# One decoder layer in fp32 on one core: side work of the first cross-attention head ordered behind its first query's split, and five weight sums of the second MLP pair given to GpSimd

## The chip, the core and the metric

The kernel runs on one core of one Trainium2 chip. The core has a matrix engine (TensorE, PE in the profile, with PEld for its weight loads), VectorE (DVE), ScalarE (ACT), GpSimd (POOL) and SyncE (SP), which here issues most DMA transfers. Matmul results land in PSUM banks, and everything else stands in SBUF or, between stages, in HBM. The metric is the device time of one execution in microseconds (us), as the median over several runs; lower is better.

## The reference

One layer over 1024 tokens of width 1024, everything in fp32: RMSNorm, a mix of mLSTM heads and forgetting-attention heads, cross-attention of 4 heads into 256 memory tokens, and an MLP with squared ReLU. Cut to what matters:

```
def cross_attention(h, memn, w_q, w_kv, w_o):
    q = (h @ w_q).reshape(B, S, X_HEADS, X_DH)          # 4 heads of 256
    k, v = jnp.split(memn @ w_kv, 2, axis=-1)
    s = jnp.einsum('bqhd,bmhd->bhqm', q, k) * (X_DH ** -0.5)
    p = jax.nn.softmax(s, axis=-1)
    o = jnp.einsum('bhqm,bmhd->bqhd', p, v).reshape(B, S, D)
    return o @ w_o

x = x + cross_attention(rmsnorm(x, ln_x), rmsnorm(mem, ln_mem), w_xq, w_xkv, w_xo)
h = rmsnorm(x, ln2)
x = x + jnp.square(jax.nn.relu(h @ w_ff1)) @ w_ff2      # 1024 -> 4096 -> 1024
```

## The kernel before

**Arithmetic.** An fp32 product is made of three faster matmuls. `split` cuts a tile into a rounded high part, written by ScalarE (L134, or L137 with a scale), and the remainder, written by VectorE (L135, L138). `mm3` then adds low x high, high x low and high x high into one PSUM bank (L186, L187, L188). So each operand passes through ScalarE and VectorE before TensorE can use it. `weights` loads a 128x1024 weight block into a "wr" buffer (two of them, L174) and splits it into "wh" and "wl" (three of each).

**Order.** The program is written as plain Python loops. A scheduler sets the order on each engine from its own estimate of times; `add_manual_dep` with NoSync binds one instruction behind another on the same engine without a semaphore. Each engine runs its instructions strictly in that order, and so does SyncE's queue of transfers.

**Cross attention.** The tokens come in two halves, `hf` 0 and 1 (512 each). For half 0, each head `hd` runs `query_whole(hd)`: the first query block (128 of the head's 256 columns) is summed in bank mm and split to r_b and r_c, the second in bank m2 (m in the profile) and split to r_p and r_a or r_y. It then runs `right_side(hd)`, which serves half 1: it loads two 128x512 rows of x1d into the two "r_f" buffers (L1190), scales them on ScalarE (L1191), and splits 128x256 pieces and differences of them (L134, L135; the differences by GpSimd in `sub`, L1353) into operands of a Strassen-like scheme of seven products. `cross_head` loads the head's keys and values (kxd L1290, vxd L1291), forms the scores in bank sc from them and the query, takes the softmax (L1303 to L1310), transposes (bank tp) and multiplies with the values (bank ov). The next head's first query again needs bank mm.

**MLP.** The first projection is done in pairs of 2x2 blocks with the same seven-product scheme. `left_up(p_, group)` prepares the weights of pair `p_` in three groups: it loads two raw blocks (odd pairs into "wr", even pairs into "z4" buffers), splits them, and forms five sums of 128x512 pieces in place, each needing the one before it. The engine for these sums is `by`. `prepare` calls it LEAD = 5 products ahead. Pairs 0 and 1 run interleaved, later pairs one by one. `left_up` for pair 1 has its first group traced in the last steps of the cross attention's output projection.

Of the kernel before, what the change touches and what calls it, by code (L numbers as in the profile page):

```python
# [44 lines left out]
def hybrid_layer(ctx: ExitStack, tc: tile.TileContext, a: dict, out: bass.AP):  # L45
    nc = tc.nc
    v, s, g = nc.vector, nc.scalar, nc.gpsimd
# [7 lines left out]
    def name(tag):  # L55
        count[0] += 1
        return f"{tag}_{count[0]}"

    def sb(tag, shape, bufs, dt=F32):
        return pool.tile(shape, dt, tag=tag, name=name(tag), bufs=bufs)  # L60

    def act(dt=F32R):
        return sb("act", [P, 8, TH], 7, dt)
# [8 lines left out]
    def w4(shape=(P, 1024), dt=F32):  # L72
        t = sb("w4", [P, 1024], 5, dt)[: shape[0]]
        return t.rearrange("p (a b) -> p a b", b=shape[2]) if len(shape) == 3 else t
# [4 lines left out]
    def w2(tag, n=512, dt=F32, p=P):  # L79
        return sb("r_" + tag, [P, 512], BUFS[tag], dt)[:p, :n]  # L80
# [6 lines left out]
    def ps_tile(tag):  # L87
        return psum.tile([P, 512], F32, tag=tag, name=name(tag), bufs=PBUFS[tag])
# [7 lines left out]
    def ov_():  # L96
        return ps_tile("ov")
# [4 lines left out]
    def mm():  # L102

        tag = banks[turn[0] % len(banks)]
        turn[0] += 1
        return ps_tile(tag)
# [24 lines left out]
    def split(hi, lo, src, scale=None):  # L131

        if scale is None:
            s.activation(hi, src, AF.Copy)  # L134
            return v.tensor_tensor(out=lo, in0=src, in1=hi.bitcast(F32), op=ALU.subtract)  # L135
        else:
            s.activation(hi, src, AF.Copy, scale=scale)  # L137
            return v.scalar_tensor_tensor(out=lo, in0=src, scalar=scale, in1=hi.bitcast(F32), op0=ALU.mult, op1=ALU.subtract)  # L138
# [5 lines left out]
    def in_order(engines=COMPUTE):  # L144
# [5 lines left out]
        for i in traced[start:]:  # L150
# [8 lines left out]
                )  # L159
            last_of[i.engine] = i.name  # L160


    def rotate(*tags):

        spare[tags] = spare.get(tags, -1) + 1
        return w2(tags[spare[tags] % len(tags)])


    def weights(src, n=1024):
        return weight_parts(weight_load(src, n))  # L170

    def weight_load(src, n=1024):
        raw = sb("wr", [P, 1024], 2)[:, :n]
        load(raw, src)  # L174
        return raw

    def weight_parts(raw):
        n = raw.shape[1]
        hi = sb("wh", [P, 1024], 3, F32R)[:, :n]
        lo = sb("wl", [P, 1024], 3, F32R)[:, :n]  # L180
        split(hi, lo, raw)
        return hi, lo

    def mm3(ps, w, x, first, last, more=False):

        nc.tensor.matmul(ps, w[1], x[0], start=first, stop=False, skip_group_check=more)  # L186
        nc.tensor.matmul(ps, w[0], x[1], start=False, stop=False, skip_group_check=more)  # L187
        nc.tensor.matmul(ps, w[0], x[0], start=False, stop=last, skip_group_check=more)  # L188

    def both(pair, f):  # L190
        return f(pair[0]), f(pair[1])
# [66 lines left out]
    def proj(w, x, tiles, kn=KT, order=None, into=None):  # L258

        wv = both(w, lambda t: t.rearrange("p (k c) -> p k c", k=kn))  # L260
        for half, n in order or [(hf, n) for n in range(tiles) for hf in range(2)]:
            ps = mm() if into is None else into
            for k in range(kn):
                mm3(ps, both(wv, lambda t: t[:, k, n * P : (n + 1) * P]), both(x[half], lambda t: t[:, k]), k == 0, k == kn - 1)
            yield n, half, ps

    VEC = {}
    at = 0
# [105 lines left out]
    z, e, q, lf = (small[:, i:j].rearrange("p (t c) -> p t c", c=c) for i, j, c in ((0, 128, GC), (128, 224, GW), (224, 320, GW), (320, 416, GW)))  # L374
# [54 lines left out]
    ps = ov_()  # L429
# [699 lines left out]
    h2 = act(), act()  # L1129
# [3 lines left out]
    def ln_x(n):  # L1133
        return vec[:, VEC["ln_x"] + n :][:, 0:1]
# [13 lines left out]
    def row_second(hf):  # L1148
        rsqrt_sums(x1_accs[hf], rcol[:, 4 * hf : 4 * hf + 4], 4)
        if hf:  # L1150
            to_row(row, rcol, 8, rowd[2:3])

    for n0 in (0, 4):
        ws = [weights(a["w_out_b"][n0 // 2 + i], 6 * P) for i in range(2)]
        for hf in range(2):
            for n in range(n0, n0 + 4):
                w = both(ws[n // 2 % 2], lambda t: t.rearrange("p (k c) -> p k c", k=3)[:, :, n % 2 * P : n % 2 * P + P])
                ps = mm()
# [12 lines left out]
    def right_room(*names):  # L1171
        t = act().rearrange("p a b -> p (a b)").rearrange("p (n q k c) -> p n q k c", n=2, q=2, k=4)
        for e, c in enumerate(names):
            R[c] = t[:, e, 0], t[:, e, 1]
        return t[:, 1]

    def cut_right(c, k, x):
        split(R[c][0][:, k], R[c][1][:, k], x)
# [3 lines left out]
    def right_side(k):  # L1182
        if not fourth:
            for c in (("11", "21"), ("t1", "t2"), ("22", "t3")):
                right_room(*c)
            fourth.append(w4((P, 4, 256)))
        x, y = w2("f"), w2("f")
        for t, n in ((x, k), (y, 4 + k)):
            with tc.issue_after(mix_done[0].ins):
                load(t, x1d[1, :, n])  # L1190
            s.activation(t, t, AF.Copy, scale=ln_x(n))  # L1191
        x1, x2, y1, y2 = (t[:, e * 256 : e * 256 + 256] for t in (x, y) for e in range(2))
        cut_right("11", k, x1)
        cut_right("21", k, y1)
        cut_right("22", k, y2)
        sub(x1, x2, x1, g)
        cut_right("t1", k, x1)
        sub(x1, y2, x1, g)
        cut_right("t2", k, x1)
        sub(x2, y2, x2, g)  # L1200
        cut_right("t3", k, x2)
        sub(fourth[0][:, k], y1, x1, g)

    def q_room(kk):
        return [rotate(*tags).bitcast(F32R) for tags in ((("b",), ("c",)), (("p",), ("a", "y")))[kk]]

    def query_whole(hd):
        q = []
        for kk in range(2):
            t = q_room(kk)  # L1210
            for _, _, ps in proj(weights(a["w_xq"][2 * hd + kk]), [h2], 1, order=[(0, 0)], into=ps_tile(("mm", "m2")[kk])):
                split(*t, ps, 1.0 / 16.0)
            q.append(t)
        return q
# [137 lines left out]
    def sub(out_, x, y, by=v):  # L1352
        by.tensor_tensor(out=out_, in0=x, in1=y, op=ALU.subtract)  # L1353
# [8 lines left out]
    def raw_pair(p_, n0, n1):  # L1362
        raws = [sb("wr", [P, 1024], 2) if p_ % 2 else z4()[:, :1024] for _ in range(2)]
        if p_ > 1:
            n0, n1 = n1, n0
        for raw, n in zip(raws, (n0, n1)):
            load(raw, a["w_ff1"][n])
        return raws[::-1] if p_ > 1 else raws
# [5 lines left out]
    def left_up(p_, group):  # L1374

        if group == 0:
            raws[p_] = raw_pair(p_, *todo[p_][2:])
        r1, r2 = raws[p_]
        x11, x12, x21, x22 = r1[:, :TH], r1[:, TH:], r2[:, :TH], r2[:, TH:]
        hi, lo = (sb(t, [P, 1024], 3, F32R) for t in ("wh", "wl"))  # L1380
        split(hi, lo, (r1, r2, r1)[group])
        if group == 0:
            h22, l22 = (w2(t, dt=F32R) for t in ("bc" if p_ else "ay"))
            split(h22, l22, x22)
            cuts[p_, 4] = both((h22, l22), lambda t: t.rearrange("p (k c) -> p k c", k=4))

            by = g if p_ > 1 else v
            by.tensor_tensor(out=x21, in0=x21, in1=x22, op=ALU.add)
            sub(x22, x21, x11, by)
            sub(x12, x12, x22, by)  # L1390
            sub(x11, h22.bitcast(F32), x22, by)
            by.tensor_tensor(out=x11, in0=x11, in1=l22.bitcast(F32), op=ALU.add)
        for e in range(2):
            cuts[p_, ((1, 2), (5, 6), (7, 3))[group][e]] = both((hi, lo), lambda t: t[:, e * TH : e * TH + TH].rearrange("p (k c) -> p k c", k=4))
        if group == 2:
            del raws[p_]
# [19 lines left out]
    def prepare(at):  # L1416
        while prep and first[prep[0]] <= at + LEAD:
            left_up(*prep.pop(0))
# [44 lines left out]
    whole = act(), act()  # L1463
    os_.append([Rows(enumerate(t[:, n] for n in range(KT))) for t in whole])
    for hd in range(XH):
        q = query_whole(hd)
        right_side(hd)
        if hd == XH - 1:
            last_room = right_room("t4")
            for k in range(4):  # L1470
                cut_right("t4", k, fourth[0][:, k])
            for _ in range(2):
                left_query(*x_prep.pop(0))
        for _ in cross_head(hd, 0, q, *os_[0]):
            pass
        if hd == 0:
            row_second(1)
    oh, ol = Rows(), Rows()
    os_.append([oh, ol])
    for hd in range(XH):  # L1480
        q = query_blocks(hd)
# [19 lines left out]
    for n in range(KT):  # L1501
        w = weights(a["w_xo"][n])
        if n == 1:
            norm_factors(0)
        if n in (1, 7):
            left_up(*prep.pop(0))
        for _, _, ps in proj(w, os_, 1, order=[(1, 0)]):
            xo_sink(n, 1, ps)
        k = n % 4
        sub(ys[0][k], ys[1][n], ys[0][k])  # L1510
        cut_h("t2" if n > 3 else "t1", 0, (k,))
# [191 lines left out]
    for at, (b, m) in enumerate(steps):  # L1703
# [16 lines left out]
        for i, of, y, op in ((1, 1, x22, ALU.add), (5, 5, x22, ALU.add), (7, 7, x22, ALU.add), (6, 6, x22, ALU.add), (2, 1, x11, ALU.add), (4, 5, x21, ALU.subtract), (3, 7, x12, ALU.subtract)):  # L1720
            if of == i:
                held[of] = bank()
            ps = held[of]
# [138 lines left out]
```

## Time and profile before

| | |
|---|---|
| median of 3 runs | 1510.02 us (1508.97 to 1510.86) |
| the profiled execution | 1511.13 us |
| its span | 1509.4 us, TensorE's granted clock 0.997 |
| TensorE busy | 1491.7 us, 99% |
| VectorE, ScalarE, GpSimd busy | 1118.6, 758.7, 525.9 us |
| cross attention's first heads | about 625 to 710 us of the span |
| start of the MLP pairs | about 855 to 900 us |

A row of a timeline gives start, duration (both us), engine, source line, operation, output <- inputs by the program's names with the buffer numbers left out, and shape; in brackets stands the idle time of the engine before it and what ended that. A row of waits gives total, count and longest in us.

### The profile page before, as it was taken

To read this page: it belongs to the slowest core of one execution; us is meant where nothing else is said; L and a number is where in the kernel's file an instruction comes from. 1 tells how busy PE (TensorE), PEld (TensorE's weight loads), DVE (VectorE), ACT (ScalarE), POOL (GpSimd) and SP (SyncE) were. 2 spreads that over 40 slices of the span, in tenths; PEclk is the share of its full clock that TensorE was granted. 3 is DMA by queue.
4 is the path that set the end of the run, shared out by engine and by line. 5 is a ranking of instruction groups with operands and counts; after the bars stand their busy time and mean duration, and the time that the engine had idled before them with its cause. 6 is when DMAs were issued, how large, how long until landed. Compare 5 with 4: busy or idle time off the path is not lost.

```text
span 1509.4 us, 22367 instructions
## 1 busy us (share of the span) xinstructions
PE 1491.7 (99%) x7806; PEld 1261.5 (84%) x7806; DVE 1118.6 (74%) x1803; ACT 758.7 (50%) x1440; POOL 525.9 (35%) x545
## 2 busy tenths in 40 slices
PE   9999999999999999999999999999999999999997
PEld 9988888889999888779988878888888888888887
DVE  7766676665788875667767899889896568887665
ACT  7324343435688764566654467566665621122134
POOL 1003130414355441623300044454544365653312
PEclk9999999999999999999999999999999999999998
DMA  6422333435777877854454447677678777776623
GB/s 235 123 77 91 99 104 126 140 127 151 254 265 258 283 245 244 269 169 126 129 186 154 147 157 278 236 260 248 217 274 296 266 273 279 279 272 251 249 85 112
DMA packets 124276, 303.04 MB, mean 201 GB/s; under 512 B 13810, under 2 KB 28460, under 8 KB 117252
## 3 DMA queue, kind: packets, MB, share of 16 engines
q1 hardware_dynamic: 124164, 301.62, 57.6%
q8 instruction: 61, 1.00, 0.3%
q14 instruction: 51, 0.42, 0.1%
HBM read 202.75 MB, written 98.82 MB: 200 GB/s over the span
## 4 chain that ended last, share of the span: by engine, by line
PE 87%; DMA 5%; DVE 3%; ACT 2%; issue 1%; POOL 1%; SPq 0%; DVEq 0%; POOLq 0%; ACTq 0%
PE tp L186 8%; PE tp L187 8%; PE tp L188 8%; PE sc L186 6%; PE sc L188 6%; PE sc L187 6%; PE m L188 5%; PE m L187 5%; PE m L186 5%; PE mm L186 5%; PE mm L188 5%; PE mm L187 5%; PE ov L807 2%; PE ov L186 2%; PE ov L187 2%; PE ov L188 2%
## 5 line engine op out<-in xcount | busy, mean ns | idle before, releaser
L186 PE MATMUL tp<-act,wl 128*128 128x512 f32 (+1 forms) x440 | 172.6, 392 | 0.0
L187 PE MATMUL tp<-act,wh 128*128 128x512 f32 (+1 forms) x440 | 172.1, 391 | 0.0
L188 PE MATMUL tp<-act,wh 128*128 128x512 f32 (+1 forms) x440 | 171.8, 391 | 0.0
L135 DVE TENSOR_TENSOR wl<-wr,wh 128x1024 fp32r<-128x1024 f32 (+2 forms) x99 | 132.2, 1335 | 28.4 <-ACT wh L134 28.1
L134 ACT ACTIVATE wh<-wr 128x1024 fp32r<-128x1024 f32 (+2 forms) x99 | 99.9, 1009 | 86.9 <-PE tp L188 32.6
L186 PE MATMUL mm<-act,wl 128*128 128x512 f32 (+1 forms) x332 | 124.1, 374 | 3.1 <-DVE r_c L138 2.7
L188 PE MATMUL mm<-act,wh 128*128 128x512 f32 (+1 forms) x332 | 123.6, 372 | 0.0
L187 PE MATMUL mm<-act,wh 128*128 128x512 f32 (+1 forms) x332 | 123.3, 372 | 0.0
L186 PE MATMUL m<-act,wl 128*128 128x512 f32 (+1 forms) x308 | 113.8, 369 | 0.8 <-DVE wl L135 0.8
L188 PE MATMUL m<-act,wh 128*128 128x512 f32 (+1 forms) x308 | 113.8, 369 | 0.0
L187 PE MATMUL m<-act,wh 128*128 128x512 f32 (+1 forms) x308 | 113.6, 369 | 0.0
L186 PE MATMUL sc<-act,wl 128*128 128x512 f32 (+1 forms) x280 | 105.6, 377 | 0.0
L188 PE MATMUL sc<-act,wh 128*128 128x512 f32 (+1 forms) x280 | 105.6, 377 | 0.0
L187 PE MATMUL sc<-act,wh 128*128 128x512 f32 (+1 forms) x280 | 105.5, 377 | 0.0
L188 PEld LDWEIGHTS tp<-act,wh 128*128 128x128 f32 x440 | 82.7, 188 | 18.9
L186 PEld LDWEIGHTS tp<-act,wl 128*128 128x128 f32 x440 | 82.7, 188 | 18.5
L187 PEld LDWEIGHTS tp<-act,wh 128*128 128x128 f32 x440 | 82.7, 188 | 18.2
L1626 POOL TENSOR_TENSOR z<-wr 128x256 f32<-128x256 f32 x56 | 51.1, 933 | 131.5 <-DMA wr<-w_ff2q 118.9
L134 ACT ACTIVATE wh<-z 128x1024 fp32r<-128x1024 f32 (+1 forms) x54 | 55.5, 1027 | 78.6 <-POOL z L1626 59.1
L135 DVE TENSOR_TENSOR wl<-z,wh 128x1024 fp32r<-128x1024 f32 (+1 forms) x54 | 77.6, 1438 | 8.2 <-ACT wh L134 8.2
L134 ACT ACTIVATE w<-wr 128x768 fp32r<-128x768 f32 (+3 forms) x35 | 28.0, 801 | 107.9 <-PE tp L188 30.4
L186 PEld LDWEIGHTS mm<-act,wl 128*128 128x128 f32 x332 | 62.4, 188 | 14.7 <-DVE r_c L138 3.1
(735 smaller groups left out, 4380.0 us busy)
## 6 DMA issues: line engine op xcount, KB each, us to landing
act<-right SPq DMA_DIRECT2D x49, 1024.0 KB
right<-w SPq DMA_DIRECT2D x56, 256.0 KB
wr<-w_ff2q SPq DMA_DIRECT2D x28, 512.0 KB
right<-r_d SPq DMA_DIRECT2D x49, 256.0 KB
right<-r_e SPq DMA_DIRECT2D x49, 256.0 KB
act<-fqk SPq DMA_DIRECT2D x48, 256.0 KB
wr<-w_in SPq DMA_DIRECT2D x20, 512.0 KB
wr<-w_ff SPq DMA_DIRECT2D x20, 512.0 KB
```

Of the source, the lines that this page charges most:

```text
L134: s.activation(hi, src, AF.Copy)
L135: return v.tensor_tensor(out=lo, in0=src, in1=hi.bitcast(F32), op=ALU.subtract)
L186: nc.tensor.matmul(ps, w[1], x[0], start=first, stop=False, skip_group_check=more)
L187: nc.tensor.matmul(ps, w[0], x[1], start=False, stop=False, skip_group_check=more)
L188: nc.tensor.matmul(ps, w[0], x[0], start=False, stop=last, skip_group_check=more)
L807: nc.tensor.matmul(self.ov[:, c0:], self.fv[:, self.j], t[:, c0:], start=self.j == 0 and t is self.p[1], stop=self.last and t is self.p[0])
L1626: g.tensor_tensor(out=o, in0=x, in1=y, op=op)
```

## The change

In the first head, `query_whole` is written out, and `right_side(0)` is traced between the first query's split and the second query. A helper `ahead_of` binds every ScalarE instruction of `right_side(0)` behind the first ScalarE instruction of that split. And `by` becomes GpSimd for pair 1 as well; only pair 0 keeps VectorE. The helper adds 16 lines, so every later line number rises by 16, and by 26 behind the loop.

```diff
+    def ahead_of(at, later_):
+        traced = nc.cur_bb.bb.instructions
+        act_ = mybir.EngineType.Activation
+        first_ = next(i for i in traced[at:] if i.engine == act_)
+        at = len(traced)
+        later_()
+        for i in nc.cur_bb.bb.instructions[at:]:
+            if i.engine == act_:
+                tc.add_manual_dep(i, first_.name, ...NoSync..., reason="ahead_of")
...
-            by = g if p_ > 1 else v
+            by = g if p_ else v
...
     for hd in range(XH):
-        q = query_whole(hd)
-        right_side(hd)
+        if hd:
+            q = query_whole(hd)
+            right_side(hd)
+        else:
+            q = [q_room(kk) for kk in range(2)]
+            w0, w1 = (weights(a["w_xq"][kk]) for kk in range(2))
+            for _, _, ps in proj(w0, [h2], 1, order=[(0, 0)], into=ps_tile("mm")):
+                traced = len(nc.cur_bb.bb.instructions)
+                split(*q[0], ps, 1.0 / 16.0)
+            ahead_of(traced, lambda: right_side(hd))
+            for _, _, ps in proj(w1, [h2], 1, order=[(0, 0)], into=ps_tile("m2")):
+                split(*q[1], ps, 1.0 / 16.0)
```

Since the scheduler works out the order anew, rows move on all engines in the cross attention's first heads and through the MLP's pairs. ScalarE at the first head, before; r_b<-mm is the first query's split, r_f are the x1d rows of `right_side(0)`, act the operands cut from them, and wh_7323 and wh_7358 the second head's weights:

```order
L1191 ACTIVATE r_f_7196<-r_f_7196,vec 128x512
L134 ACTIVATE wh_7323<-wr_7321 128x1024
L1191 ACTIVATE r_f_7197<-r_f_7197,vec 128x512
L134 ACTIVATE act_7192<-r_f_7196 128x256
L222 ACTIVATE r_c_7106<-r_p_7102 128x512
L134 ACTIVATE act_7192<-r_f_7197 128x256
L134 ACTIVATE act_7194<-r_f_7197 128x256
L134 ACTIVATE act_7193<-r_f_7196 128x256
L134 ACTIVATE act_7194<-r_f_7196 128x256
L137 ACTIVATE r_b_7122<-mm_7130 128x512
L134 ACTIVATE wh_7358<-wr_7356 128x1024
```

And ScalarE there in the changed kernel:

```order
L134 ACTIVATE wh_7323<-wr_7321 128x1024
L238 ACTIVATE r_c_7106<-r_p_7102 128x512
L137 ACTIVATE r_b_7122<-mm_7138 128x512
L1207 ACTIVATE r_f_7169<-r_f_7169,vec 128x512
L1207 ACTIVATE r_f_7170<-r_f_7170,vec 128x512
L134 ACTIVATE wh_7358<-wr_7356 128x1024
L134 ACTIVATE act_7165<-r_f_7169 128x256
L134 ACTIVATE act_7165<-r_f_7170 128x256
L134 ACTIVATE act_7167<-r_f_7170 128x256
L137 ACTIVATE r_p_7124<-m_1363_7191 128x512
```

The split moved ahead of the x1d rows' scaling and cuts, and the cuts now stand behind wh_7358. SyncE's transfers for the second head, before (r_f_7389 and r_f_7390 are its two x1d rows, w its keys and values, wr_7531 a later query's weights):

```order
L1290 DMA w_1364_7218<-kxd 128x1024
L1291 DMA w_1365_7219<-vxd 128x1024
L1190 DMA r_f_7389<-x1d 128x512
L1290 DMA w_1399_7411<-kxd 128x1024
L1291 DMA w_1400_7412<-vxd 128x1024
L174 DMA wr_7531<-w_xq 128x1024
L1190 DMA r_f_7390<-x1d 128x512
```

And in the changed kernel:

```order
L190 DMA wr_7531<-w_xq 128x1024
L1306 DMA w_1364_7218<-kxd 128x1024
L1307 DMA w_1365_7219<-vxd 128x1024
L1206 DMA r_f_7389<-x1d 128x512
L1206 DMA r_f_7390<-x1d 128x512
L1306 DMA w_1399_7411<-kxd 128x1024
L1307 DMA w_1400_7412<-vxd 128x1024
```

The two rows of x1d now follow each other, and the w_xq transfer went ahead of the first head's keys. GpSimd in the changed kernel at the start of the MLP; wr_9374 and wr_9375 are pair 1's raw weights, z_1761 is pair 2's:

```order
L1404 TENSOR_TENSOR wr_9375<-wr_9375 128x512
L1369 TENSOR_TENSOR wr_9375<-wr_9375,wr_9374 128x512
L1369 TENSOR_TENSOR wr_9374<-wr_9374,wr_9375 128x512
L1369 TENSOR_TENSOR wr_9374<-r_b_9382,wr_9375 128x512
L1408 TENSOR_TENSOR wr_9374<-wr_9374,r_c_9383 128x512
L1404 TENSOR_TENSOR z_1761_9612<-z_1761_9612 128x512
```

The first five of these rows are new on GpSimd; before, its queue had only the last one here, and the five stood on VectorE among the rows ahead of the split wl_9433<-z_1680_9101 (the last of them behind it).

More of the change, by code (lines that the diff above doesn't have):

```diff
@@ L160, in in_order @@
             last_of[i.engine] = i.name
+    def ahead_of(at, later_):
[6 more added lines that the diff above has]
+            if i.engine == act_:
+                tc.add_manual_dep(
+                    i,
+                    first_.name,
+                    mybir.DependencyInfo(mybir.DependencyClass.NoSync, mybir.DependencyReason.DATA),
+                    reason="ahead_of",
+                )
     def rotate(*tags):
```

## The prediction

> **What bounds the kernel.** I read the page first, then TensorE's waits, then the timelines of the engines on which those waits end.
>
> ```profile
> span 1509.4 us, 22367 instructions
> PE 1491.7 (99%) x7806; PEld 1261.5 (84%) x7806; DVE 1118.6 (74%) x1803; ACT 758.7 (50%) x1440; POOL 525.9 (35%) x545
> ...
> PE mm L186 <- DVE r_c L138: 2.7, 1, 2.7
> ...
> PE m L186 <- DVE wl L135: 0.8, 1, 0.8
> PE sc L186 <- DVE r_c L138: 0.7, 1, 0.7
> ...
> PE mm L186 <- DVE wl L135: 0.4, 1, 0.4
> ```
>
> The first row is the span; the second gives busy time, share and count by engine. TensorE (PE) works 99% of the span, and the change takes no matmul away, so it can only win or lose at TensorE's waits. The four rows of waits (total, count, longest, in us) are those that the change can touch. Here they are in time:
>
> ```profile
> 633.08 0.40 PE L186 MATMUL m<-act,wl 128*128 128x512 f32 x1
> ...
> 641.54 0.50 PE L186 MATMUL mm<-act,wl 128*128 128x512 f32 x1 [2.70 <-DVE r_c L138]
> ...
> 655.74 0.39 PE L186 MATMUL sc<-w,r_c 128*128 128x256 f32 x1
> ...
> 673.51 0.38 PE L186 MATMUL sc<-w,r_c 128*128 128x256 f32 x1 [0.68 <-DVE r_c L138]
> ...
> 704.97 0.38 PE L186 MATMUL mm<-act,wl 128*128 128x256 f32 x1 [0.43 <-DVE wl L135]
> ...
> 869.54 0.50 PE L186 MATMUL m<-act,wl 128*128 128x512 f32 x1 [0.83 <-DVE wl L135]
> ```
>
> The bracket is the idle time before a row and what ended it. 641.54 is the second head's first query, kept out of bank mm until VectorE has read the first head's query there; 655.74 begins the second head's scores, 673.51 the third's; 869.54 is the first MLP pairs' second group. The most that can be won here is 2.70 + 0.68 + 0.43 + 0.83 = 4.64 us, 0.31% of the span.
>
> **Part one, the first head's side work behind its first split.** TensorE turns to the second query at 633.08, so the first query's sum in mm is complete then. This is what ScalarE does with it:
>
> ```profile
> 632.18 0.72 ACT L1191 ACTIVATE r_f<-r_f,vec 128x512 f32<-128x512 f32 x1 [1.10 <-DMA r_f<-x1d]
> ...
> 634.71 0.72 ACT L1191 ACTIVATE r_f<-r_f,vec 128x512 f32<-128x512 f32 x1 [0.85 <-DMA r_f<-x1d]
> ...
> 638.62 0.42 ACT L134 ACTIVATE act<-r_f 128x256 fp32r<-128x256 f32 x1 [1.74 <-POOL r_f L1353]
> 639.55 0.42 ACT L134 ACTIVATE act<-r_f 128x256 fp32r<-128x256 f32 x1 [0.52 <-POOL r_f L1353]
> 640.00 0.60 ACT L137 ACTIVATE r_b<-mm 128x512 fp32r<-128x512 f32 x1
> 640.49 1.05 ACT L134 ACTIVATE wh<-wr 128x1024 fp32r<-128x1024 f32 x1
> ...
> 640.81 0.68 DVE L138 SCALAR_TENSOR_TENSOR r_c<-mm,r_b 128x512 fp32r<-128x512 f32 x1
> ```
>
> The split r_b<-mm starts only at 640.00, behind the side work, which waits for a load and for GpSimd. In the changed order it can start soon after 633.1, r_c follows within 1.5 us, and mm is free long before TensorE comes at 638.84 (641.54 less 2.70). I take the whole 2.70 off.
>
> The side work does not vanish, it is late next. Its splits now stand behind wh<-wr, which needs a w_xq load and ran here at 640.49. The three 128x256 splits and the GpSimd chain behind them took from 638.62 to the end of the last subtraction near 641.5; now they begin when wh<-wr ends, about 641.4, so the r_f buffers come free near 644.1, some 2.6 us later. On these buffers the second head hangs:
>
> ```profile
> 641.50 0.32 SPq L1190 DMA_DIRECT2D r_f<-x1d  x1
> ...
> 643.34 0.60 SPq L1190 DMA_DIRECT2D r_f<-x1d  x1
> ...
> 644.66 0.72 ACT L1191 ACTIVATE r_f<-r_f,vec 128x512 f32<-128x512 f32 x1 [1.38 <-DMA r_f<-x1d]
> ...
> 650.42 0.72 ACT L1191 ACTIVATE r_f<-r_f,vec 128x512 f32<-128x512 f32 x1 [2.79 <-DMA r_f<-x1d]
> ...
> 654.37 0.59 ACT L137 ACTIVATE r_b<-mm 128x512 fp32r<-128x512 f32 x1
> ...
> 654.99 0.69 DVE L138 SCALAR_TENSOR_TENSOR r_c<-mm,r_b 128x512 fp32r<-128x512 f32 x1
> ```
>
> SPq is SyncE's queue of issues. Of the second head's two x1d loads the first was used 3.16 us after issue (644.66 less 641.50), the second 7.08 (650.42 less 643.34), because kxd, vxd and w_xq were issued between them. The new order issues the two next to each other, before kxd and vxd, the w_xq load having moved ahead. Issued at about 644.5, with some 4.2 us for it (between 3.16 and 7.08, nearer the first, as nothing large is now issued in front of it), the second is used near 648.7, 1.7 earlier than 650.42. The second head's r_c then ends near 655.68 less 1.7, at 654.0. TensorE, which found r_c done 0.06 before 655.74, comes 2.70 earlier, at 653.0. So there is a new wait of about 1.0 at the second head's scores. Its bounds: 0, if the loads land as fast as the first did and the softmax rows do not get in front of the split; 5.3, if all of this merely moves 2.6 later, the second load again issued 1.84 behind the first and taking 7.08 (2.7 + 2.6).
>
> The kxd and vxd loads now go out behind r_f, some 3 us later than at 641.9; with the 7.08 as the longest transfer time of these rows they are in by 652.2, ahead of the scores that read kxd at 653.0, so I cost them nothing; that cover is 0.8.
>
> The third head's 0.68: its r_b<-mm stood behind the scaling of the last x1d row, and now that row stands behind the split. The 0.43 at 704.97 is a wl split at the end of the same stretch, behind side work that ends earlier. I take both off, −1.1, the weakest term of the sum; bound 0, if TensorE's earlier arrival eats what is won.
>
> **Part two, pair 1's sums.** VectorE in the 13 us before the 0.83:
>
> ```profile
> 855.71 0.68 DVE L1388 TENSOR_TENSOR wr<-wr 128x512 f32<-128x512 f32 x1
> 856.83 1.23 DVE L135 TENSOR_TENSOR wl<-wr,wh 128x1024 fp32r<-128x1024 f32 x1 [0.44 <-ACT wh L134]
> ...
> 861.05 0.69 DVE L1353 TENSOR_TENSOR wr<-wr,wr 128x512 f32<-128x512 f32 x1
> ...
> 865.86 0.69 DVE L1353 TENSOR_TENSOR wr<-wr,wr 128x512 f32<-128x512 f32 x1
> 866.46 0.69 DVE L1353 TENSOR_TENSOR wr<-r_b,wr 128x512 f32<-128x512 f32 x1
> ...
> 868.27 1.22 DVE L135 TENSOR_TENSOR wl<-z,wh 128x1024 fp32r<-128x1024 f32 x1
> ```
>
> From 856.83 to the end of 868.27 VectorE has no gap (no bracket in that stretch), and 868.27 is the split for which TensorE waits: each microsecond added or removed ahead of it is TensorE's. Rows follow each other 0.60 apart (865.86 to 866.46), so the three L1353 rows that leave are worth 1.80. The L1388 row is followed by a 0.44 wait for ScalarE and gives nearly nothing; the fifth sum, L1392, stood behind the critical split.
>
> In exchange GpSimd runs five sums in a chain beside these rows. What that costs VectorE is shown later, where pairs 2 and up do it already:
>
> ```profile
> L1353 POOL TENSOR_TENSOR wr<-wr,wr x22: 1280/1298/1675, 682.7 to 1147.9; 128x512 f32<-128x512 f32 x22
> ...
> L1353 DVE TENSOR_TENSOR w<-w x14: 681/1177/1405, 895.1 to 1157.1; 128x512 f32<-128x512 f32 x14
> ...
> L1353 DVE TENSOR_TENSOR w<-w,w x6: 679/685/687, 824.5 to 877.1; 128x512 f32<-128x512 f32 x6
> ...
> 899.14 1.40 POOL L1388 TENSOR_TENSOR z<-z 128x512 f32<-128x512 f32 x1 [3.44 <-DMA z<-w_ff]
> ...
> 899.30 2.32 DVE L135 TENSOR_TENSOR wl<-z,wh 128x1024 fp32r<-128x1024 f32 x1
> ...
> 873.06 3.59 POOL L1388 TENSOR_TENSOR z<-z 128x512 f32<-128x512 f32 x1 [129.08 <-DMA z<-w_ff]
> ```
>
> The first three are groups (count, ns min/median/max, first and last start). One GpSimd sum takes 1.30. VectorE's 128x512 subtraction takes 0.685 where GpSimd is idle and 1.18 in the median where it works, and the 128x1024 split 2.32 instead of 1.23 when a GpSimd sum began 0.16 before it: up to 1.1 us for each sum that meets a VectorE row at its start. VectorE is gap-free here and nearly all its rows read SBUF only, so the chained sums meet a row each time. I take 1.1 for the three subtractions and the last addition, all of which must lie ahead of 868, and 0.4 for the first, 4 x 1.1 + 0.4 = 4.8. Less 1.8, TensorE's wait grows by 3.0, from 0.83 to about 3.8. Bounds: with the median stretch, 5 x 0.5 − 1.8 = +0.7; with no stretch −0.83, since no more than the wait can go; with a fifth full stretch 5.5 − 1.8 = +3.7. Behind the chain on GpSimd stands pair 2's first sum, which started at 873.06, some 5 us after the chain should be done, so nobody waits for that.
>
> The row at 873.06 is against this: there GpSimd took 3.59 for a 1.30 sum and VectorE was not held up. The Trainium skill (SBUF — State Buffer, "Who interferes with whom") says that VectorE's two-input operation on SBUF and GpSimd's access share a port pair as an exclusive lock, whoever starts first holding it for the whole instruction. The 2.32 row agrees; by that rule the stage loses 3.0, by the 873.06 row alone it gains 0.83. The rows of the MLP stage are many and the other is one, after 129 us of idle GpSimd, so I keep the first.
>
> **The MLP stage after that.** Its rows are re-ordered on all engines, pairs 2 and up unchanged in work:
>
> ```profile
> 900.00:1190.00 290.00, 290.00 (x1245) 233.27 (x1244) 248.39 (x275) 188.42 (x296) 132.45 (x89) 1.00 0.75 262
> ```
>
> The columns are length, then busy time of PE, PEld, DVE, ACT and POOL. TensorE is busy 290.00 of 290.00, so a new order can only add. I take 0.6, between the two nearest waits for a weight split (0.43 and 0.83); bounds 0 and their sum, 1.3.
>
> **The sum.** −2.7 − 1.1 + 1.0 + 3.0 + 0.6 = +0.8 us. The profiled execution took 1511.13 (span 1509.4 and 1.7 around it), so it would become 1511.9; on the median of the runs, 1510.02, that is 1510.8. A time cannot be told from no change within 0.2%, 3.0 us: below 1507.0 is faster, above 1513.0 slower.
>
> **The rivals.**
> 1. GpSimd's sums cost VectorE nothing. For it: the 873.06 row, and five sums fit in the 13 us. Against it: the 2.32 and 1.18 rows. Then the 0.83 goes and the later order costs nothing: −2.7 − 1.1 + 1.0 − 0.8 = −3.6, 1506.4.
> 2. The wait of part one is handed on whole to the second head, and slower comes out. Place: its scores, waiting for r_c behind the second x1d load. If its issue and its 7.08 us are as before, only later, the wait is 5.3 and not 1.0: 0.8 + 4.3 = +5.1, 1515.1. For it: r_f is free 2.6 later, and w_xq is still issued close by. Against it: nothing now stands between the two loads. It decides from the point where r_c ends 2.2 us later than the 654.0 above, at 656.2, since 0.8 + 2.2 = 3.0.
> 3. Part one gains nothing, because the split waits elsewhere, say for its q buffers. Nothing shows r_b or r_c in use at 633; the row at 640.00 has no wait of its own. Then the sum is 0.8 + 2.7 − 1.0 = +2.5, 1512.5.
>
> **How the numbers follow.** The forecast 0.57, the first rival 0.23, the second 0.14, the third 0.06. The forecast's own range is 1508 (median stretch, no new order cost: 0.8 − 2.3 − 0.6 = −2.1) to 1513 (+1.3 of head wait and +0.7 of stretch or of order). Reaching below the first rival's time, and towards the second's up to where its wait is 4.5, gives 1505.9 to 1514.3, which leaves out about 0.1 of the second rival and as much of the first. Faster: most of the first rival and a sliver of the forecast, 0.22. Slower: the second rival and the upper edge of the forecast and the third, 0.17. Same: 0.61.
>
> **What the changed profile would show.** The 2.7 wait of mm for r_c is gone and r_b<-mm of the first head starts near 633.5. A wait of sc for r_c of about 1 stands near 653, and the second head's two r_f loads are issued within 0.5 of each other. Near 855 to 866 five GpSimd sums on wr of 1.3 stand beside 128x512 VectorE rows of 1.2 to 1.8, and the wait of m for wl near 867 is 3 to 4. If those VectorE rows stay at 0.69, rival 1 holds; if sc waits 3 or more, rival 2. The forecast fails most easily on how many of the five sums VectorE really meets.

## The result and the profile after

The changed kernel took 1516.87 us in the median of 6 runs (1514.84 to 1519.91), the kernel before 1509.38 (1507.93 to 1510.86): a ratio of 1.0051, interval [1.004, 1.0061]. It is 7.5 us slower, where 0.8 was forecast and 1514.3 was the upper end. The profiled execution was the longest of the six, 1519.91. Its page and the waits of TensorE (total, count, longest):

```profile
span 1518.2 us, 22377 instructions
PE 1494.3 (98%) x7806; PEld 1263.7 (83%) x7806; DVE 1121.9 (74%) x1798; ACT 758.0 (50%) x1440; POOL 537.9 (35%) x550
...
PE tp L202 <- DVE r_f L1568: 4.5, 2, 2.5
PE m L202 <- DVE wl L135: 2.6, 1, 2.6
...
PE sc L202 <- DVE r_c L138: 1.4, 1, 1.4
PE sc L202 <- DVE r_f L1568: 1.2, 1, 1.2
...
PE m L202 <- DVE r_f L1568: 0.7, 1, 0.7
PE tp L202 <- ACT row L1581: 0.6, 1, 0.6
```

The 2.7 at L186 for r_c is gone, and so are the 0.7 and the 0.4 of the first heads. The first pairs' wait for wl grew from 0.8 to 2.6, with 0.65 more for row beside it. What nobody had foreseen are the rows with r_f L1568, VectorE's additions that empty a PSUM bank in the MLP's pairs. TensorE's timeline shows where they stand:

```profile
867.78 0.50 PE L202 MATMUL m<-act,wl 128*128 128x512 f32 x1 [2.56 <-DVE wl L135]
956.56 0.50 PE L202 MATMUL tp<-act,wl 128*128 128x512 f32 x1 [2.00 <-DVE r_f L1568]
1018.38 0.50 PE L202 MATMUL sc<-act,wl 128*128 128x512 f32 x1 [1.22 <-DVE r_f L1568]
1078.16 0.50 PE L202 MATMUL m<-act,wl 128*128 128x512 f32 x1 [0.72 <-DVE r_f L1568]
1139.76 0.50 PE L202 MATMUL tp<-act,wl 128*128 128x512 f32 x1 [2.53 <-DVE r_f L1568]
```

They come every 60 us, once in three pairs (their products are 252 matmuls apart, and a pair has 84), and make 6.47 in all. Before, TensorE had no wait above 0.15 us from 870 to 1498. The account of waits is then: first heads 1.38 − 3.81 = −2.43, first pairs 0.65 + 2.56 − 0.83 = +2.38, later pairs +6.47; together +6.4.

The span grew by 8.8, so some 2.4 us are no waits; TensorE's busy time grew by 2.6. TensorE's clock accounts for that. The stretches of 2 us behind the 2.56 wait (length, then busy time and count of PE, PEld, DVE, ACT, POOL; the third number from the end is the granted clock):

```profile
868.00:870.00 2.00, 2.00 (x8) 1.58 (x8) 2.00 (x4) 0.98 (x2) 0.00 (x0) 0.80 0.64 184
870.00:872.00 2.00, 2.00 (x6) 1.54 (x6) 2.00 (x5) 1.23 (x4) 0.79 (x1) 0.50 0.19 78
872.00:874.00 2.00, 2.00 (x9) 1.65 (x8) 2.00 (x3) 1.10 (x3) 2.00 (x1) 0.85 0.28 105
874.00:876.00 2.00, 2.00 (x11) 1.59 (x10) 2.00 (x4) 0.53 (x1) 0.89 (x1) 1.00 0.94 253
```

The clock falls to half for about 3.4 us, worth (0.20 + 0.50 + 0.15) x 2 = 1.7 us. The same happens behind the 2.00 wait at 956, but not behind the 2.53 at 1139. The two together cost 3.4, so some 0.8 of it came back in rows that no wait shows. In the profile before it happens nowhere in this part, not even behind the 2.70 wait.

### The profile page after: what moved, and what is told of

Same layout as the page of the kernel before. It is cut to its first block, busy times and chain, and to the rows that moved or that the text cites. A ratio compares the mean times of both kernels' runs of the same rounds, so it can differ in the third digit from the quotient of the medians.

```text
span 1518.2 us, 22377 instructions
## 1 busy us (share of the span) xinstructions
PE 1494.3 (98%) x7806; PEld 1263.7 (83%) x7806; DVE 1121.9 (74%) x1798; ACT 758.0 (50%) x1440; POOL 537.9 (35%) x550
## 4 chain that ended last, share of the span: by engine, by line
PE 81%; DMA 7%; DVE 7%; ACT 2%; issue 2%; POOL 1%; SPq 0%; DVEq 0%; POOLq 0%; ACTq 0%
PE tp L202 7%; PE tp L204 7%; PE tp L203 7%; PE sc L202 5%; PE m L202 5%; PE sc L203 5%; PE sc L204 5%; PE m L203 5%; PE m L204 5%; PE mm L202 5%; PE mm L204 5%; PE mm L203 5%; PE ov L823 2%; PE ov L202 2%; PE tp L804 2%; PE ov L203 2%
## 5 line engine op out<-in xcount | busy, mean ns | idle before, releaser
L204 PEld LDWEIGHTS mm<-act,wh 128*128 128x128 f32 x332 | 62.4, 188 | 11.6
```

## The experiments

Several experiments bind an engine to a given order in the MLP stage: a table lists the instructions of that stage, and each is tied behind the one before it on its engine, without a semaphore:

```diff
+    for e_, steps in PINNED.items():
+        ...
+            if prev_ is not None:
+                tc.add_manual_dep(i_, prev_, ...NoSync..., reason="pinned")
```

Part two alone gives the MLP stage the same order as both parts, part one alone that of before, so the two parts' orders are separate. Ratios below are to the kernel before on the same chip, with 95% intervals.

**The two parts apart.** Part one keeps `by = g if p_ > 1 else v`; part two is that line alone:

```diff
-            by = g if p_ > 1 else v
+            by = g if p_ else v
```

> Part one alone (the first head's side work behind its split; pair 1's sums stay on VectorE). The order of the MLP stage is then that of before on every engine. Theory: part one does what was forecast and touches nothing later. In the changed kernel the waits 2.70, 0.68 and 0.43 of the first heads were gone and one of 1.38 had come, so this kernel should be 2.4 us faster than before, about 1507.0, with the 0.83 at the first MLP pairs unchanged. Rival (the loss of the whole change starts in the first heads): 1510 or more.

> Part two alone (pair 1's five sums on GpSimd). Theory: all of the loss is here. The waits of the changed kernel that are new from 855 us on are 0.65 + 2.56 - 0.83 = 2.4 at the first pairs and 2.00 + 1.22 + 0.72 + 2.53 = 6.5 for VectorE's L1542 rows (which empty PSUM banks) later, and TensorE's clock falls for some us after one or two of the waits, 1 to 2 us more: 9 to 11 us slower than before, about 1519. Rival: the two parts make the loss only together, then less than 1515.

Part one alone took 1506.25, ratio 0.9977 [0.9968, 0.9987], 3.4 us faster; in its profile the two waits left are 0.93 (sc for r_c) and 0.88 (m for wl). Part two alone took 1518.60, ratio 1.0056 [1.0044, 1.0068], 8.5 us slower. All of the loss is in part two, as expected. The two sum to +5.1, while the whole change measured +7.7 [6.0, 9.2] by its ratio; but part one's interval is −4.8 to −2.0 and part two's +6.6 to +10.3, so that anything beyond a plain sum is not shown.

**The sums' engine against the order.** The first kernel is part two with all engines bound in the order of before, so that only the five sums change engine; the second is the mirror, the sums left on VectorE and all engines bound in the order that part two gets:

```diff
 e3: by = g if p_ else v      PINNED = order of before (PE, DVE, ACT, POOL, SP)
 e4: by = g if p_ > 1 else v  PINNED = order of part two (PE, DVE, ACT, POOL, SP)
```

> Part two with the order of before: the five sums stand on GpSimd, ahead of pair 2's first sum, and all other instructions from the first MLP pairs to the end of the MLP's first projection are bound on every engine in the order in which before has them. Theory (the 6.5 us come from the new order): the four later waits are gone, the wait at the first pairs is 2 to 4 instead of 0.83, 1 to 4 us slower than before, 1510.5 to 1513.5. Rival (GpSimd's sums hold VectorE up and the delay is carried through the stage): the later waits stay, 1516 or more. If the sums cost VectorE nothing: 1508.5 to 1509.5.

> The order alone: pair 1's five sums stay on VectorE as before, and all other instructions of the MLP stage are bound on every engine in the order that the scheduler gives them with the sums on GpSimd (part two alone). Theory (order): the later waits for L1542 rows, 6.5 us in all, are there without any sum on GpSimd, 1514.5 to 1518. Rival (GpSimd's sums): no such waits, 1509 to 1511.

The sums alone took 1513.00, ratio 1.0023 [1.0014, 1.0031], +3.5 us; no wait for L1542 is in the profile, and the first pairs wait 0.53 and 2.56. The order alone took 1515.83, ratio 1.0034 [1.0021, 1.0047], +5.1 us, and without any sum on GpSimd it has the waits of the later pairs, 3.3 us in all in its profile where 6.5 were expected, the last like this:

```profile
1133.31 0.50 PE L186 MATMUL tp<-act,wl 128*128 128x512 f32 x1 [1.99 <-DVE r_f L1542]
```

The two effects add (3.5 + 5.1 = 8.6 against 8.5 for part two). So GpSimd's sums cost some 3.5 [2.1, 4.7] and the new order 5.1 [3.2, 7.1]: both are clear of no change, and the order is the greater by its median, though the intervals overlap.

**Both parts, order of before.**

```diff
 e7: both parts               PINNED = order of before (PE, DVE, ACT, POOL, SP)
```

> Both parts, with the MLP stage bound on every engine in the order of before (the five sums on GpSimd). Theory (two separate effects, no more): part one's -3.3 and the sums' +3.4 add to about nothing, 1508.5 to 1511, with waits of sc for r_c near 1 and of m for wl near 2.6 and no wait for L1568 rows. Rival (the parts worsen each other, as 7.5 for both against -3.3 and +9.0 apart would not show): 1513 or more, or the first pairs' wait is another.

1509.75, ratio 0.9999 [0.999, 1.0008]. TensorE's waits are 1.15 for r_c, 0.57 for row and 2.55 for wl, and none later. Part one's gain and the sums' price cancel; this is the change as the forecast had summed it without its term for the new order (−2.7 − 1.1 + 1.0 + 3.0 = +0.2). Here is VectorE ahead of the 2.55 wait, and GpSimd beside it:

```profile
855.33 1.78 DVE L1369 TENSOR_TENSOR w<-r_e,w 128x512 f32<-128x512 f32 x1
857.03 1.79 DVE L1369 TENSOR_TENSOR r_d<-r_e,r_d 128x512 f32<-128x512 f32 x1
858.74 1.78 DVE L135 TENSOR_TENSOR act<-r_f,act 128x512 fp32r<-128x512 f32 x1
860.45 1.78 DVE L135 TENSOR_TENSOR act<-r_d,act 128x512 fp32r<-128x512 f32 x1
862.15 0.68 DVE L135 TENSOR_TENSOR act<-r_e,act 128x512 fp32r<-128x512 f32 x1
...
850.92 1.30 POOL L1404 TENSOR_TENSOR wr<-wr 128x512 f32<-128x512 f32 x1 [111.18 <-DMA r_p<-x1d]
855.03 3.24 POOL L1369 TENSOR_TENSOR wr<-wr,wr 128x512 f32<-128x512 f32 x2 [2.81 <-DVE r_c L135]
858.22 1.75 POOL L1369 TENSOR_TENSOR wr<-r_b,wr 128x512 f32<-128x512 f32 x1
860.05 1.62 POOL L1408 TENSOR_TENSOR wr<-wr,r_c 128x512 f32<-128x512 f32 x1
```

Four chained sums, and beside them exactly four VectorE rows of 1.78 instead of 0.68: the engines take turns, and the row after the last sum is 0.68 again. The first sum at 850.92 costs nothing, since VectorE was waiting for ScalarE then. 4 x 1.1 − 1.8 = +2.6 was to be expected from this, and +2.2 stands in the waits (0.57 + 2.55 − 0.88). The exclusive lock of the Trainium skill (SBUF — State Buffer, "Who interferes with whom") agrees with these four rows.

**Which queue.** The chain behind the 2.00 wait at 956 in the changed kernel, in order of time, on four engines:

```profile
939.06 0.33 SPq L1383 DMA_DIRECT2D z<-w_ff  x1
940.22 0.32 SPq L1609 DMA_DIRECT2D right<-r_p  x1
...
946.41 0.60 ACT L1581 ACTIVATE r_p<-ov 128x512 f32<-128x512 f32 x1 [2.63 <-DMA right<-r_p]
...
947.05 0.69 DVE L1568 TENSOR_TENSOR w<-sc,r_p 128x512 f32<-128x512 f32 x1 [2.52 <-ACT r_p L1581]
...
955.82 0.68 DVE L1568 TENSOR_TENSOR r_f<-tp,r_p 128x512 f32<-128x512 f32 x1
```

And the same store, refill and bank in the kernel before, with TensorE's next product in that bank:

```profile
933.26 0.32 SPq L1583 DMA_DIRECT2D right<-r_p  x1
...
942.78 0.58 ACT L1555 ACTIVATE r_p<-ov 128x512 f32<-128x512 f32 x1
...
954.04 0.69 DVE L1542 TENSOR_TENSOR r_f<-tp,r_p 128x512 f32<-128x512 f32 x1
...
957.43 0.39 PE L186 MATMUL tp<-act,wl 128*128 128x512 f32 x1
```

The store of r_p to `right` went out at 933.26 before and at 940.22 after; ScalarE refills the buffer r_p and now waits 2.63 for that store, VectorE waits 2.52 for ScalarE, and the bank that TensorE wants is emptied late. In SyncE's new order the store stands behind a load of w_ff1, in four of the pairs, right where the four waits are. The load does not hold up the store's issue: in both kernels the store leaves 0.03 us after VectorE's remainder r_p<-r_p has ended (940.19 and 933.23). What is longer behind the load is the transfer: ScalarE got the buffer 4.97 to 6.81 us after the issue in the four places.

TensorE's own order has moved too. Before, it came to bank tp 2.70 us after the bank was empty (957.43 less 954.73); in the changed kernel it came at 954.56 and the bank was empty only at 956.50. In each of the four places the product that waits and its neighbour, 12 matmuls of 2.80 us together, have changed places, so that the bank is wanted 2.80 earlier in the order. All four waits are shorter than that. No run moves TensorE's products by themselves, so that this share of the waits is read from the rows and not shown by an experiment.

Two first tries on the store: the store moved five rows up in SyncE's queue, to where before has it, and SyncE's new order put into the kernel before. ("Own order" means that a kernel is bound in the order that the scheduler gave it.)

```diff
 e5: both parts, own order    SP: store right<-r_p 5 rows earlier, in 4 places
 e6: kernel before, own order SP: order of part two
```

> The changed kernel (both parts) with its own order bound on every engine, but four of SyncE's transfers moved: the store right<-r_p of the second and later pairs stands, in four places, five rows earlier in SyncE's queue, ahead of the load of w_ff1 (into z or wr) behind which the changed order has put it. Theory (that store is issued late, ScalarE waits for buffer r_p, VectorE behind it, and the bank is emptied late): the four later waits for VectorE's L1568 rows, 6.5 us in all, are gone, and with them some of the clock's loss; 1508.5 to 1512. Rival (another engine's order, or GpSimd's sums, make these waits): 1515 to 1518 as the changed kernel.

> The kernel before, all engines bound in its own order in the MLP stage, but SyncE's queue in the order that part two gave it; no sum is moved. Theory (SyncE's order is enough): waits for L1542 rows of 3 to 6 us in all appear, 1513 to 1517. Rival (it takes the other engines' order too): 1509 to 1511.

Both came out far slower than either theory had it: 1534.13, ratio 1.0155 [1.014, 1.0171], and 1535.35, ratio 1.0174 [1.0161, 1.0188]. In the first the moved store waited at the head of SyncE's queue for the remainder r_p<-r_p, which VectorE forms late in its own new order, and held back the stores behind it:

```profile
939.93 0.32 SPq L1609 DMA_DIRECT2D right<-r_p  x1
...
944.36 0.64 ACT L134 ACTIVATE r_d<-w 128x512 fp32r<-128x512 f32 x1 [4.24 <-DMA right<-r_d]
...
1087.73 0.80 PE L202 MATMUL m<-act,wl 128*128 128x512 f32 x1 [3.79 <-DVE r_f L1568]
```

The other has such waits with other buffers, ending in one of TensorE's of 8.00 at 1194. They show that a queue's order must fit the order of the engines that feed it; they do not tell which row of the new order is at fault. So the next three move fewer rows:

```diff
 e9:  both parts, own order    DVE: r_p<-r_p ahead of the second wl split, 4 places
                               SP: store right<-r_p ahead of the w_ff1 load, 4 places
 e10: kernel before, own order the reverse: r_p<-r_p behind the second wl split, store behind the load
 e11: both parts, own order    SP: store right<-r_p ahead of the w_ff1 load, 4 places
```

> The changed kernel with its own order bound on every engine, but four rows of VectorE and four of SyncE moved: the remainder r_p<-r_p of a pair's right-hand side stands ahead of the second of the two wl splits behind which the new order has put it, and the store right<-r_p that it feeds stands ahead of the load of w_ff1, one or two rows earlier. Theory (this remainder comes 6 us late, its store lands late, ScalarE waits for buffer r_p, VectorE behind it, and a PSUM bank is emptied late): the four waits for L1568 rows, 6.5 us, are gone, and so is some of the clock's loss; 1509 to 1511.5, as both parts in the order of before. Rival (the other rows of the new order make these waits): 1514 or more.

> The kernel before with its own order bound, but the same four remainders r_p<-r_p put behind the second wl split, and the four stores right<-r_p behind the load of w_ff1; no sum moved, nothing else. Theory: four waits for L1542 rows of 1 to 3 us appear, 1512.5 to 1517. Rival (the other rows of the new order make them): none, 1509 to 1511.

> The changed kernel with its own order bound, but the four stores right<-r_p put ahead of the load of w_ff1 (SyncE alone; the remainder on VectorE stays late). Theory (the remainder is the late one, and the store waits for it wherever it stands): the four waits stay, 1515 to 1519. Rival (the load in front of the store is the cause): waits gone, 1509 to 1512.

With both moves 1513.66, ratio 1.0024 [1.0014, 1.0035], between what the theory and its rival had; with the store alone 1513.69, ratio 1.0027 [1.0016, 1.0038], clear of the changed kernel's [1.004, 1.0061]. So 3.2 us of the changed kernel's 1516.87 hang on the store's place, one or two rows, and VectorE's remainder adds nothing; the theory written for the last one was wrong and its rival half right. ScalarE's wait for that store is gone; it has the buffer no later than 3.22 to 3.48 us after the issue:

```profile
937.90 0.32 SPq L1609 DMA_DIRECT2D right<-r_p  x1
...
941.12 0.58 ACT L1581 ACTIVATE r_p<-ov 128x512 f32<-128x512 f32 x1
...
1006.12 0.69 DVE L135 TENSOR_TENSOR w<-w,r_e 128x512 fp32r<-128x512 f32 x1 [2.43 <-POOL r_f L1369]
...
1072.26 0.50 PE L202 MATMUL m<-act,wl 128*128 128x512 f32 x1 [0.54 <-DVE r_f L1568]
```

Three waits for L1568 of 0.5 to 0.8 are left. The reverse in the kernel before gave 1510.17, ratio 1.0005 [0.9996, 1.0014]: no such wait. A late store alone costs nothing there: ScalarE waits 0.78 for it, but the row has slack behind it, the bank tp is empty at 954.39 all the same, and TensorE comes to it only at 956.84. The order as a whole has to be tight for it to matter.

The row at 1006.12 suggested the rest: VectorE waits 2.43 for GpSimd in front of a row that empties a bank. The last two move that row ahead:

```diff
 e13: as e11, and DVE: L1568 r_p<- two rows earlier, 4 places
 e14: both parts, own order    DVE: L1568 r_p<- two rows earlier, 4 places
```

> The changed kernel with its own order bound, the four stores right<-r_p ahead of the load of w_ff1 as in e11, and on VectorE in four places the L1568 row r_p<- that empties a PSUM bank moved two rows ahead, in front of the remainder w<-w that waits for GpSimd (1.2 to 2.4 us in e11). Theory (these two places in the queues make the four later waits): the waits for L1568 rows, 2.1 us in e11, are below 0.5 in sum, 1509 to 1511.5. Rival (the rest of the order matters as much): they stay, 1512.5 or more.

> The changed kernel with its own order bound, and only the four L1568 rows r_p<- moved two rows ahead on VectorE; the stores right<-r_p stay behind the load of w_ff1. Theory (two places, each with its share): ScalarE still waits for buffer r_p, but the bank is emptied some 1.3 us earlier in each place, so that the four waits fall from 6.5 to about 2 to 3; 1512 to 1515. Rival (only the store counts): no change, 1515 to 1518.

1513.18, ratio 1.0025 [1.0016, 1.0034], and 1514.46, ratio 1.0032 [1.0021, 1.0043]. With the store there is no gain over e11 to be told (four waits of 0.56 to 0.70 remain), so this theory of the rest is wrong. Without it some 2 us are gained, but its interval reaches that of the changed kernel. What makes the last 3.5 us between these kernels and the one in the order of before is not settled by a run. Their waits for L1568 make 2.1 to 2.6 of it. The rows above point to the products that changed places on TensorE, since each of these waits is under 2.80; but TensorE's order was not tried by itself, since e5 and e6 had shown what a mixture of orders does.

**Two ways to go on from part one.** Two of pair 1's sums moved on VectorE behind the split for which TensorE waits, the rest in the order of before; and part one's edit for the second head too:

```diff
 e8:  part one                DVE: L1369 wr<-wr,wr and wr<-r_b,wr behind L135 wl<-z
 e12: part one
-        if hd:
+        if hd > 1:
```

> Part one alone, and instead of giving pair 1's sums to GpSimd two of them (the second and third subtraction) stay on VectorE but stand behind the split wl<-z for which TensorE waits 0.88, not ahead of it; everything else in the MLP stage bound in the order of before. Theory: that split comes 1.2 earlier, the 0.88 wait goes, nothing else needs the two sums soon: 0.9 faster than part one alone, about 1505.4, and the fastest of all. Rival (another row is late instead): 1506.3 or more, with a new wait of TensorE between 865 and 885 us.

> Part one alone, done for the second head as well (its side work bound behind its first query's split). Theory (the second head's new wait of 0.9 to 1.4 for r_c comes from side work in front of that split): the wait goes, 1 us faster than part one alone, about 1505.2. Rival (it is handed on to the third head, or the new order of the later heads brings its own waits): 1506 or more.

The first took 1505.23, ratio 0.9974 [0.9965, 0.9983], the lowest median of all. The 0.88 wait is gone from its list and nothing has come in its place between 865 and 885:

```profile
PE sc L202 <- DVE r_c L138: 2.2, 1, 2.2
PE ov L129 <- POOL ident L118: 1.9, 1, 1.9
PE mm L229 <- DVE c_r L1794: 1.6, 1, 1.6
```

But the second head's wait was 2.15 in that execution (0.22 to 1.4 in the others with part one), and against part one alone the intervals overlap. The second head's edit took 1511.39, ratio 1.0014 [1.0005, 1.0023], 5 us slower than part one alone: the second head's wait of sc for r_c was 0.22, which e13 and e14 have without this edit, and later heads have new ones,

```profile
PE ov L265 <- DVE rcol L224: 1.9, 1, 1.9
...
PE sc L202 <- DVE r_c L138: 0.9, 2, 0.7
...
PE sc L202 <- DVE r_y L138: 0.8, 1, 0.8
```

which stand from 687 to 702. So the edit loses by new waits in later heads, and that it shortened the second head's is not shown.

## Why the prediction was wrong

- **The 2.70 goes: right.** In the six profiles without part one this wait was 1.77 to 3.81, so that the 2.70 was one draw of it. The first head's split and remainder, and what follows on ScalarE, in the changed kernel:

```profile
632.68 0.60 ACT L137 ACTIVATE r_b<-mm 128x512 fp32r<-128x512 f32 x1 [1.11 <-PE mm L204]
...
636.02 1.06 ACT L134 ACTIVATE wh<-wr 128x1024 fp32r<-128x1024 f32 x1 [0.53 <-DMA wr<-w_xq]
...
635.10 0.69 DVE L138 SCALAR_TENSOR_TENSOR r_c<-mm,r_b 128x512 fp32r<-128x512 f32 x1
...
643.35 0.94 SPq L1206 DMA_DIRECT2D r_f<-x1d  x2
```

- **The side work late, the second head waits 1.0: right, 1.38.** The split wh<-wr, which I had taken to start at 640.5 as before, started at 636.0; the second head's two loads went out together at 643.35, not 644.1 and 644.5. Over the executions with part one this wait was 0.22 to 2.15.
- **The 0.68 and 0.43 go: right** in the changed kernel. With the 2.70 and the new wait part one is worth −2.4 in its waits, against −2.8 in the forecast, and −3.4 measured alone.
- **Pair 1's sums, +3.0: right in kind and near in size**: +2.4 in waits, +3.5 measured alone, in which the clock's loss behind the 2.56 wait can have a share. GpSimd's rows do hold VectorE up, four times 1.1; the row of 3.59 at 873.06, which spoke against it, was no guide.
- **The MLP stage after that, +0.6 with 1.3 as its bound: this step failed.** It measured 6.5 in waits and 1.7 in clock in the profiled execution, and 5.1 by the run of the order alone. I had bounded it by two waits from elsewhere (0.43 and 0.83), which say nothing of what a new order of queues can do. That TensorE was busy 290.00 of 290.00 us said only that a new order could not win, not how little slack there was; VectorE was busy 248.4 of these 290 and SyncE's queue carried stores that buffers wait for. The runs show in its place: the store right<-r_p moved behind a load in four pairs, worth 3.2 us, and should have been priced as the second head's loads were. The rest of the order's price is argued from the traces alone: TensorE wants four banks one product earlier.
- **What the sum did not have at all:** a wait can cost more than its length, by the clock.
- **The rivals:** none of the three came. The change came out slower by a fourth way, in the term held smallest.

## What to carry to other kernels

An edit that gives a few rows to another engine can make the scheduler order a whole stage anew, and that can be worth as much as the rows or more (here 5.1 us against 3.5). Where the order changes, go through every queue that frees a buffer, stores above all, price each one that moved behind a load, and see whether TensorE now wants a bank sooner; a bound taken from other waits is none. To know what an edit itself costs, bind the order of before and run it so.

## What the runs showed of the hardware that was not expected

- TensorE's clock can halve for about 3.4 us behind a wait, at a loss of 1.7 us. The same wait of 2.54 to 2.56 at the first pairs was followed by it in the profiles of six kernels (the changed one, e2, e5, e7, e9, e13) and not in those of three (e3, e11, e14); a wait of 1.99 had it (e4), one of 2.70 not (before). The six runs of the changed kernel had mean granted clocks of 0.995 to 0.997, and the two at 0.995 were the longest.
- What decides can be read from the traces: not the length of the wait alone, but where it falls. The half clock began at 869.18 and at 957.93 in the changed kernel, 26 times 3.413 us apart. If the span is laid out in stretches of 3.413 us from there, and likewise in the other profiles, half clock began in 20 places, each right behind a stretch in which TensorE idled 1.72 to 3.17 us. Of the stretches at full clock that were not followed by it, one had 1.87 (e14) and all others at most 1.63, the end of the program left out. The wait of 2.53 was cut at 1138.83 into 1.61 and 0.92, the 2.70 before into 1.63 and 1.07. Where the bounds fall differs from one profile to the next, so a wait of some 2 to 3 us may or may not cost the 1.7.
- The Trainium skill (TensorE: Matmul & The Clock Gate, "What's actually happening") has the clock at half after an idle window of about 3.4 us. The half clock agrees with the rows at 868 to 874; an idle time of a whole such window was not needed here, where 1.72 to 3.17 us in one were enough.
